# Row factors by transposes, idle transposes in a second place, and forget rates from quarters of the array, in a two-layer decoder on one Trainium2 core

## The chip, the cores and the metric

The kernel runs on one core of a Trainium2 chip. The core has a matrix engine (TensorE, "PE" in the profile, with its weight loads as "PEld"), a vector engine (DVE), an activation engine (ACT), a general engine (POOL) and a queue engine that issues transfers (SP). The metric is device time in microseconds of one execution, the lower the better. Three timed runs of the kernel before are shown, and one profiled execution.

## The reference

Two decoder layers over 256 positions of width 1024, float32 throughout. What matters here:

```
hn = rmsnorm(h, norm_mix_g[layer])        # every sublayer starts with one
h  = h + mixer(hn)                        # layer 0: stick-breaking + MoBA heads, layer 1: forgetting attention
h  = h + memory_cross_attention(rmsnorm(h), rmsnorm(mem))
h  = h + conv_ffn(rmsnorm(h))             # 1024 -> 2*2816, conv of width 3, silu gate, 2816 -> 1024
return rmsnorm(h)

# forgetting attention, layer 1: 16 forget rates per position come out of the same input projection
f_logit = proj[..., 3*D_MODEL:] + b_f     # (256 positions, 16 heads)
log_f   = log_sigmoid(f_logit);  c = cumsum(log_f)
s = q.k*scale + c[t] - c[s]
```

`rmsnorm(x, g) = x * rsqrt(mean(x*x) + 1e-6) * g`: one factor per position.

## The kernel before

**Layout.** h lies transposed: eight tiles `h[k]` of 128 features by 256 positions (two halves of 128). A product of a weight matrix with h is a projection of 24 matmuls: for each of the eight k-tiles, weights and activations are split into a high and a low part (`hi`, `lo`, a rounded float32 and its rest), and three products are summed, (hi, xh), (hi, xl), (lo, xh). Such a projection is `proj` (out has 128 features on the partitions) or `proj_nat` (positions on the partitions; the moving operand is then the weights). Operands of these matmuls have the type fp32r, one pass each. A plain float32 matmul is carried out as two passes, each with a weight load of its own, and shows as two instructions in the trace.

**Weights.** `block` (L119) loads 128x1024 weights (SP queue), rounds them on ACT (L127) and takes the rest on DVE (L128). PE's instructions stand in the order in which the code issues them; the order on the other engines comes from a scheduler that uses priorities.

**Row factors.** The norm is applied late: projections run on h times g alone, and their results are multiplied by the factor per position. `Stats.sums` (L254) sums squares over features with plain float32 matmuls of one column (L259), takes mean and epsilon (L262, DVE), and the power -0.5 on POOL (L266): the result is `rcol`, 128 positions by 2. It then builds a diagonal matrix `dg` from `rcol` with two DVE operations (L269). `Stats.spread` (L272) multiplies the diagonal by a matrix of ones with one plain float32 matmul of 256 columns (L274), so that every partition holds all 256 factors, and copies them to `row` (L277, ACT). Results are multiplied by `row` where they leave PSUM. There are seven spreads: at the start of layer 0, for the memory, and for cross attention and feed-forward network of both layers and the mixer of layer 1. Where a projection is given `hooks={n: f}`, f is issued behind its n-th product.

**Forget rates.** In layer 1, before q and k of the first group, L639 runs a `proj` with m=16: 24 matmuls of 16 output features. `decay_rows` (L493) turns them into cumulative sums, and each head loads its row from DRAM (`bc`).

**Feed-forward network** (`ffn`, L772): 22 pairs of up-projections, f = 0 to 21. The sums come behind product 6 of the first projection of f = 1, the spread behind product 12 of the second. Behind f = 1 stands `pace` (L522): six transposes of the identity into a spare PSUM bank whose result nobody reads. `renorm` (L775) makes normed activations `xn` (POOL, ACT, DVE) that replace raw ones from f = 4 (RAW) on. From f = 2 to the end of the up-projections PE runs 20 x 2 x 24 = 960 products, and in layer 0 another 8 x 66 = 528 of the down-projection behind them.

**Heads.** `visit(n)` issues a pair of heads at set ticks between projections: `heads_out` of pair n-2 (L418, outputs of 64 partitions per head), score products, `weigh` of pair n-1 (for softmax heads six transposes, L404), then the scores. `cross` issues its score products (L699, contraction over 64 rows per head) and outputs (L755, 64 partitions per head) in plain float32.

Of the kernel before, what the change touches and what calls it, by code (L numbers as in the profile page):

```python
# [72 lines left out]
def trunk(ctx: ExitStack, tc: tile.TileContext, a: dict, out: bass.AP):  # L73
# [145 lines left out]


    class Stats:
        def __init__(self, keep="", one=False):
# [31 lines left out]
        def sums(self):  # L254
            if self.ssq is None:
                ps = self.ps = bank(psA, "acc")
                for t in range(2):
                    for i, p in enumerate(self.parts):
                        nc.tensor.matmul(ps[:, 2 * t:2 * t + 1], p[:, t * P:(t + 1) * P], ones[:, 0:1], start=i == 0,  # L259
                                         stop=i == len(self.parts) - 1)  # L260
            ms = tiny.tile([P, 2], F32, tag="ms", name="ms")
            nc.vector.tensor_scalar(ms, ps[:, 0:4:2] if self.ssq is None else self.ssq, 1.0 / D, EPS, op0=ALU.mult,  # L262
                                    op1=ALU.add)
            bufs = 1 if self.keep else 2
            self.col = tiny.tile([P, 2], F32, tag="rcol" + self.keep, name="rcol", bufs=bufs)
            nc.gpsimd.tensor_tensor(self.col, ms, half, op=ALU.pow)  # L266
            self.dg = tmp.tile([P, T], F32, tag="diag", name="diag", bufs=1)
            for t in range(2):
                nc.vector.tensor_scalar(self.dg[:, t * P:(t + 1) * P], ident, self.col[:, t:t + 1], None, op0=ALU.mult)  # L269


        def spread(self, ps=None):  # L272
            ps = ps or self.ps
            nc.tensor.matmul(ps[:, :T], ones, self.dg, start=True, stop=True)  # L274
            bufs = 1 if self.keep else 2
            self.row = act.tile([P, T], F32, tag="rrow" + self.keep, name="rrow", bufs=bufs)
            nc.scalar.copy(self.row, ps[:, :T])  # L277


    def proj(b, off, xs, ps, first=True, last=True, m=P, hooks={}):  # L280
        n = 0
        for k, (xh, xl) in enumerate(xs):
            s = slice(off + k * m, off + k * m + m)
            end = last and k == len(xs) - 1
            for w, x in ((b.hi, xh), (b.hi, xl), (b.lo, xh)):
                nc.tensor.matmul(ps[:m], w[:, s], x, start=first and n == 0, stop=end and w is b.lo)  # L286
                n += 1
                if n in hooks:
                    hooks[n]()
        return ps  # L290

# [201 lines left out]
    def decay_rows(ps, st):  # L493
        f = lambda n: xin.tile([P, T], F32, tag="gh", name=n, bufs=NG)[:16]
        x, e, u, w, one, c = (f(f"f{n}") for n in "xeuw1c")
        nc.gpsimd.memset(one, 1.0)
        nc.vector.tensor_mul(x, ps[:16], st.row[:16])
        nc.vector.tensor_scalar(x, x, small[:16, C_BF:C_BF + 1], None, op0=ALU.add)
# [20 lines left out]
        return rows  # L519


    def pace():  # L522
        ps = bank(psO, "po")
        for i in range(6):
            nc.tensor.transpose(ps[:, (i % 4) * P:(i % 4 + 1) * P], ident, ident)

# [26 lines left out]
    def mixer(layer, st, xs):  # L553
# [14 lines left out]
        def visit(n):  # L568
            if n >= 2:
                outs[n - 2] = heads_out(heads[n - 2], pairs[n - 2][2], (n % 2) * P)  # L570
            if layer == 0:
                if n == 2:
                    rope_tables()
            if n < 8:
                q, k, _, rows = pairs[n]
                heads[n] = [Stick(i, q, k) if layer == 0 and n < 4 else Soft(i, q, k, rows[i]) for i in range(2)]
                both_products(heads[n])
            if 1 <= n < 9:
                for hd in heads[n - 1]:
                    hd.weigh()  # L580
            if n < 8:
                for hd in heads[n]:
                    hd.scores()
            if layer == 0 and n == 4:
                mem.sums()
            if layer == 0 and n == 5:
                mem.spread(accA())
            if layer == 0 and n == 1:
# [5 lines left out]
        for g in range(4):  # L594
# [43 lines left out]
            elif g == 0:  # L638
                f = proj(block(a["fox_f"], 8 * 16), 0, xs, bank(psO, "po", T), m=16)  # L639
                q, more = pair(0, ({3: st.sums}, {3: st.spread}))  # L640
                k = more()
                decay = decay_rows(f, st)
                q, k = evac_row(q, st, "q", True), evac_row(k, st, "k", False)
            else:
# [12 lines left out]
            for t in range(2):  # L657
                v.append(evac_col(proj_nat(b, xs, t, accA()), st, t, "v", 6))
                pipe.tick()
# [111 lines left out]

    def ffn(layer, st, xs):  # L772
        gs = []
        base = C_CONV + layer * 4 * 2 * KF
# [36 lines left out]
        for f in range(KF):  # L811
# [3 lines left out]
            for i in range(2):  # L815
                if f == 0:
                    pss.append(first[i])
                    continue
                hooks = ({6: st.sums}, {12: st.spread})[i] if f == 1 else {}
                acc = (accS, accA)[n % 7 % 2]()  # L820
# [8 lines left out]
            if f == 1:  # L829
                pace()  # L830
                renorm()
# [13 lines left out]
    def down_rows(gs):  # L845
# [21 lines left out]
        def finish(t):  # L867
            both = tiny.tile([P, 4], F32, tag="ssq", name="ssq")
            ms, col = both[:, 2:3], both[:, 3:4]
            for c in range(2):  # L870
                nc.scalar.activation(wide("sq"), acc[t][c], AF.Square, accum_out=both[:, c:c + 1])
            o = [wide("out") for _ in range(2)]
            if t:
                nc.vector.tensor_mul(o[0], acc[t][0], gain[0])
            nc.vector.tensor_add(ms, both[:, 0:1], both[:, 1:2])
            nc.vector.tensor_scalar(ms, ms, 1.0 / D, EPS, op0=ALU.mult, op1=ALU.add)
            nc.gpsimd.tensor_tensor(col, ms, half[:, 0:1], op=ALU.pow)
# [37 lines left out]
def _layout(inp):  # L915
# [27 lines left out]
    d["fox_in"] = qkv(fox[:, :3 * D])  # L943
    d["fox_f"] = c(kt(fox[:, 3 * D:]).reshape(P, -1))
    for n, w in (("ab_out", inp["ab_w_out"][0]), ("fox_out", inp["fox_w_out"][0])):
# [51 lines left out]
```

## Time and profile before

| what | value |
|---|---|
| timed runs | 671.16, 675.79, 671.14 us; median 671.16 us |
| profiled execution | 671.95 us, of which the span from the first to the last instruction is 670.2 us |
| PE busy | 660.1 us, 98% of the span |
| DVE, ACT, POOL busy | 528.5, 434.7, 60.0 us |
| mean granted TensorE clock | 0.997 of full speed |

In the rows below, a line of the timeline begins with its start in us, then its length, engine, source line (L286 is line 286 of the kernel), operation, output<-inputs by the program's names, shape and count. A matmul's length is its latency; what it costs PE in a stream is the time from one start to the next. A timeline row with x8 merges eight like instructions. In the chain of waits a piece is start, length and what ran, with its number of instructions.

### The profile page before, as it was taken

The numbers are of one execution on the slowest core, as the hardware profiler recorded it, in microseconds if no ns is written. First come the engines' busy times: TensorE is split into PE (matmuls) and PEld (weight loads), VectorE is DVE, ScalarE is ACT, GpSimd is POOL, SyncE is SP. The second block draws the span as 40 slices with busy tenths as digits, with TensorE's granted clock in tenths as the row PEclk, the third lists the DMA queues.
The fourth block names the chain that finished last, engine by engine and source line by source line (L and its number), as shares of the span: only waits on it lengthen the run. The fifth ranks groups of instructions, "written<-read, shape, count | busy, mean of one in ns | idle before, by whom it ended". The sixth has DMA issues, their size and how long they took to land.

```text
span 670.2 us, 14201 instructions
## 1 busy us (share of the span) xinstructions
PE 660.1 (98%) x5467; PEld 630.6 (94%) x5467; DVE 528.5 (79%) x1086; ACT 434.7 (65%) x864; POOL 60.0 (9%) x72
## 2 busy tenths in 40 slices
PE   8999999999999999999999999999999999999996
PEld 6999999989999999999999999999999999998884
DVE  5877995899999999766486787578999999994442
ACT  6699774767777776544464686567776777763332
POOL 0001110306100000011100000021350000000000
PEclk9999999999999999999999999999999999999998
DMA  8976451545455665665558554326356666654501
GB/s 293 400 270 227 130 205 34 187 158 184 147 200 197 217 219 174 185 190 181 192 186 268 188 173 132 126 76 208 88 197 215 193 219 205 207 193 151 191 0 64
DMA packets 39076, 121.83 MB, mean 182 GB/s; under 512 B 4944, under 2 KB 8928, under 8 KB 39008
## 3 DMA queue, kind: packets, MB, share of 16 engines
q1 hardware_dynamic: 38720, 120.62, 54.8%
q8 instruction: 43, 0.70, 0.4%
q10 hardware_dynamic: 288, 0.30, 0.1%
q14 instruction: 25, 0.20, 0.1%
HBM read 118.79 MB, written 1.06 MB: 179 GB/s over the span
## 4 chain that ended last, share of the span: by engine, by line
PE 91%; DVE 4%; issue 2%; DMA 1%; ACT 1%; SPq 0%; POOLq 0%; POOL 0%; DVEq 0%
PE acc L286 40%; PE sc L286 24%; PE acc L300 7%; PE sc L861 4%; PE po L861 2%; PE acc L861 2%; DVE wlo L128 2%; PE po L418 2%; PE sc L619 1%; PE sc L377 1%; PE sc L404 1%; PE po L300 1%; DVE xl L179 1%; DMA raw<-ab_first 1%; PE sc L699 1%
## 5 line engine op out<-in xcount | busy, mean ns | idle before, releaser
L128 DVE TENSOR_TENSOR wlo<-raw,whi 128x512 fp32r<-128x512 f32 (+2 forms) x285 | 262.2, 939 | 61.7 <-ACT whi L127 59.4
L127 ACT ACTIVATE whi<-raw 128x512 fp32r<-128x512 f32 (+2 forms) x285 | 225.2, 821 | 105.8 <-PE acc L286 46.4
L286 PE MATMUL sc<-xn,whi 128*128 128x256 f32 x672 | 116.1, 276 | 0.0
L286 PEld LDWEIGHTS sc<-xn,whi 128*128 128x128 f32 x672 | 101.3, 188 | 0.2
L286 PE MATMUL sc<-xn,wlo 128*128 128x256 f32 x336 | 92.7, 276 | 0.0
L286 PE MATMUL acc<-xn,whi 128*128 128x256 f32 x480 | 83.1, 276 | 0.0
L286 PE MATMUL acc<-xh,whi 128*128 128x256 f32 x288 | 81.8, 284 | 0.0
L286 PE MATMUL acc<-xl,whi 128*128 128x256 f32 x288 | 80.1, 278 | 0.0
L286 PE MATMUL acc<-xh,wlo 128*128 128x256 f32 x288 | 80.1, 278 | 0.0
L286 PEld LDWEIGHTS acc<-xn,whi 128*128 128x128 f32 x480 | 72.3, 188 | 0.0
L286 PE MATMUL acc<-gh,whi 128*128 128x256 f32 x240 | 67.2, 280 | 0.0
L286 PE MATMUL acc<-gl,whi 128*128 128x256 f32 x240 | 66.9, 279 | 0.1
L286 PE MATMUL acc<-gh,wlo 128*128 128x256 f32 x240 | 66.6, 277 | 0.0
L286 PE MATMUL acc<-xn,wlo 128*128 128x256 f32 x240 | 66.2, 276 | 0.0
L286 PEld LDWEIGHTS sc<-xn,wlo 128*128 128x128 f32 x336 | 63.1, 188 | 0.0
L234 POOL TENSOR_TENSOR sq<-sq 128x256 f32<-128x256 f32 x33 | 27.7, 838 | 328.1 <-ACT sq L228 313.5
L286 PEld LDWEIGHTS acc<-xl,whi 128*128 128x128 f32 x288 | 54.3, 189 | 0.1
L286 PEld LDWEIGHTS acc<-xh,whi 128*128 128x128 f32 x288 | 54.3, 188 | 0.2
L286 PEld LDWEIGHTS acc<-xh,wlo 128*128 128x128 f32 x288 | 54.2, 188 | 0.0
L286 PEld LDWEIGHTS acc<-gh,whi 128*128 128x128 f32 x240 | 45.2, 188 | 0.9 <-ACT gh L174 0.8
L286 PEld LDWEIGHTS acc<-gl,whi 128*128 128x128 f32 x240 | 45.1, 188 | 0.5 <-DVE gl L175 0.5
L286 PEld LDWEIGHTS acc<-gh,wlo 128*128 128x128 f32 x240 | 45.1, 188 | 0.0
(253 smaller groups left out, 1496.3 us busy)
## 6 DMA issues: line engine op xcount, KB each, us to landing
raw<-up SPq DMA_DIRECT2D x88, 512.0 KB, 4.3
raw<-fox_in SPq DMA_DIRECT2D x24, 512.0 KB, 4.2
raw<-down_rows SPq DMA_DIRECT2D x22, 512.0 KB, 4.3
raw<-ab_in SPq DMA_DIRECT2D x20, 512.0 KB, 6.7
raw<-down SPq DMA_DIRECT2D x16, 448.0 KB, 3.3
raw<-ab_out SPq DMA_DIRECT2D x8, 512.0 KB, 4.2
raw<-down SPq DMA_DIRECT2D x8, 512.0 KB, 3.6
raw<-fox_out SPq DMA_DIRECT2D x8, 512.0 KB, 3.4
```

Of the source, the lines that this page charges most:

```text
L127: i = nc.scalar.activation(hi[:, s], raw[:, s], AF.Copy)
L128: j = nc.vector.tensor_sub(lo[:, s], raw[:, s], hi[:, s].bitcast(F32))
L179: nc.vector.scalar_tensor_tensor(lo, src, g, hi.bitcast(F32), op0=ALU.mult, op1=ALU.subtract))
L234: nc.gpsimd.tensor_tensor(sq, sq, self.acc, op=ALU.add)
L286: nc.tensor.matmul(ps[:m], w[:, s], x, start=first and n == 0, stop=end and w is b.lo)
L300: nc.tensor.matmul(ps, x[:, s], y[:, w], start=n == 0, stop=n == 3 * KD - 1)
L377: nc.tensor.matmul(s[:, c], q[:, qs], k[:, 0:n], start=i == 0, stop=True, skip_group_check=True)
L404: nc.tensor.transpose(self.s[:, c:c + P], self.p[:, c:c + P], ident)
L418: nc.tensor.matmul(po[i * DH:(i + 1) * DH, q], v[m][:, vc + i * DH:vc + (i + 1) * DH], hd.pt[:, c], start=m == 0, stop=m == 1)
L619: nc.tensor.matmul(ps, wt[:, o + i * P:o + (i + 1) * P], x, start=start, stop=n == KD - 1 and wt is b.lo)
L699: nc.tensor.matmul(s[:, t * T:(t + 1) * T], self.q[:, t * P:(t + 1) * P], self.k, start=t == 0, stop=True, skip_group_check=True)
L861: nc.tensor.matmul(acc[t][c], x[:, s], y[:, c * 512:(c + 1) * 512], start=False, stop=k == KF - 1 and x is gl, skip_group_check=True)
```

## The change

It has these parts:

1. `sums` no longer builds the diagonal. `spread` issues two transposes of 128 columns: the stationary operand is a column of `rcol`, repeated over 128 columns, the moving one the identity. `turns(ps, n)` issues n idle transposes of the identity ahead of them: none in most places, two in the mixer of layer 1, four in the feed-forward networks.
2. In the feed-forward network the spread stands behind product 11 instead of 12, and `pace` (six idle transposes as before) behind product 21 of the same projection instead of behind its end.
3. The forget rates: weights `fw` (32 columns per k-tile, 16 of them zeros) are loaded once and multiplied by g during layer 0 (`gate_weights`); `gates` issues eight plain float32 matmuls of 32 output rows straight from h, the k-tile k going to rows 32*(k%4) of one PSUM bank, so that four quarters of the array's columns are used in turn. One ACT copy and three DVE additions sum the quarters. `gates` and then `sums` stand behind product 20 of q, the spread behind product 15 of k. The v results of the first group go to another PSUM pool (`accS`).
4. `rope_tables` moves behind `weigh` in its visit, the memory's spread ahead of `weigh` in its visit.
5. At the end, the mean's scale and epsilon are applied to the first half of the sum while the second is still made, and one fused operation follows in place of two.

```
+    def turns(ps, n):
+        for i in range(n):
+            c = slice(i % 2 * P, (i % 2 + 1) * P)
+            nc.tensor.transpose(ps[:, c], ident, ident)
+    def pace():
+        turns(bank(psO, "po", T), 6)
...
-            self.dg = tmp.tile([P, T], F32, tag="diag", name="diag", bufs=1)
-            for t in range(2):
-                nc.vector.tensor_scalar(self.dg[:, t * P:(t + 1) * P], ident, self.col[:, t:t + 1], None, op0=ALU.mult)
-        def spread(self, ps=None):
+        def spread(self, ps=None, idle=0):
             ps = ps or self.ps
-            nc.tensor.matmul(ps[:, :T], ones, self.dg, start=True, stop=True)
+            turns(ps[:, T:], idle)
+            for t in range(2):
+                nc.tensor.transpose(ps[:, t * P:(t + 1) * P], self.col[:, t:t + 1].broadcast_to([P, P]), ident)
...
+    fw = cst.tile([P, KD, 32], F32, name="fw")
+    def gate_weights():
+        nc.sync.dma_start(fw, a["fox_f"])
+        g = small[:, G_MIX + KD:G_MIX + 2 * KD]
+        nc.vector.tensor_tensor(fw, fw, g.unsqueeze(2).broadcast_to([P, KD, 32]), op=ALU.mult)
+    def gates(ps):
+        for k in range(KD):
+            j = 32 * (k % 4)
+            nc.tensor.matmul(ps[j:j + 32], fw[:, k], h[k], start=k < 4, stop=k > 3, skip_group_check=True)
...
-        nc.vector.tensor_mul(x, ps[:16], st.row[:16])
+        nc.scalar.copy(x, ps[:16])
+        for j in (32, 64, 96):
+            nc.vector.tensor_add(x, ps[j:j + 16], x)
+        nc.vector.tensor_mul(x, x, st.row[:16])
...
-                f = proj(block(a["fox_f"], 8 * 16), 0, xs, bank(psO, "po", T), m=16)
-                q, more = pair(0, ({3: st.sums}, {3: st.spread}))
+                f = bank(psO, "po", T)
+                def rates():
+                    gates(f)
+                    st.sums()
+                q, more = pair(0, ({20: rates}, {15: lambda: st.spread(idle=2)}))
...
-                hooks = ({6: st.sums}, {12: st.spread})[i] if f == 1 else {}
+                hooks = ({6: st.sums}, {11: lambda: st.spread(idle=4), 21: pace})[i] if f == 1 else {}
...
             if f == 1:
-                pace()
                 renorm()
...
+            nc.vector.tensor_scalar(ms, both[:, 0:1], 1.0 / D, EPS, op0=ALU.mult, op1=ALU.add)
             if t:
                 nc.vector.tensor_mul(o[0], acc[t][0], gain[0])
-            nc.vector.tensor_add(ms, both[:, 0:1], both[:, 1:2])
-            nc.vector.tensor_scalar(ms, ms, 1.0 / D, EPS, op0=ALU.mult, op1=ALU.add)
+            nc.vector.scalar_tensor_tensor(ms, both[:, 1:2], 1.0 / D, ms, op0=ALU.mult, op1=ALU.add)
```

How instructions move, in three places. On PE at the start of layer 1's mixer, before (po is the bank of the forget rates, acc that of q, sq the squares):

```order
L286 MATMUL po<-xl,whi 16x256
L286 MATMUL po<-xh,wlo 16x256
L286 MATMUL acc<-xh,whi 128x256
L286 MATMUL acc<-xl,whi 128x256
L286 MATMUL acc<-xh,wlo 128x256
L259 MATMUL acc<-const,sq 128x1 x2
L286 MATMUL acc<-xh,whi 128x256
```

And with the change, 20 products into q:

```order
L295 MATMUL acc<-xl,whi 128x256
L313 MATMUL po<-h_97,fw 32x256 x2
L313 MATMUL po<-h_98,fw 32x256 x2
L313 MATMUL po<-h_99,fw 32x256 x2
L313 MATMUL po<-h_100,fw 32x256 x2
L268 MATMUL acc<-const,sq 128x1 x2
L295 MATMUL acc<-xh,wlo 128x256
```

The 24 matmuls ahead of q (the last two are seen above) are gone, and eight stand inside q, ahead of the sums.

On PE in a feed-forward network with the change, in the second projection of f = 1 (the x4 and x6 rows are idle transposes):

```order
L295 MATMUL acc<-xl,whi 128x256
L224 MATMUL acc<-const 128x128 x4
L283 MATMUL acc<-const,rcol 128x128 x2
L295 MATMUL acc<-xh,wlo 128x256
...
L224 MATMUL po<-const 128x128 x6
L295 MATMUL acc<-xh,whi 128x256
```

The first block of six replaces one L274 row; the row of x6 was behind the projection's last product and is now three products ahead of its end.

On DVE in the same network while `xn` is made, before (u and c belong to the convolution; the second xn row here is the last of the eight):

```order
L793 TENSOR_TENSOR u<-acc,rrow 128x256
L128 TENSOR_TENSOR wlo<-raw,whi 128x1024
L179 SCALAR_TENSOR_TENSOR xn<-hr,small,xn 128x256
L128 TENSOR_TENSOR wlo<-raw,whi 128x1024
L179 SCALAR_TENSOR_TENSOR xn<-hr,small,xn 128x256
```

And with the change:

```order
L820 TENSOR_TENSOR u<-acc,rrow 128x256
L128 TENSOR_TENSOR wlo<-raw,whi 128x1024
L179 SCALAR_TENSOR_TENSOR xn<-hr,small,xn 128x256 x2
L823 SCALAR_TENSOR_TENSOR c<-u,small,c 128x255 x2
L823 SCALAR_TENSOR_TENSOR c<-u,small,c 128x254
L179 SCALAR_TENSOR_TENSOR xn<-hr,small,xn 128x256
L823 SCALAR_TENSOR_TENSOR c<-u,small,c 128x254
L820 TENSOR_TENSOR u<-sc,rrow 128x256
L128 TENSOR_TENSOR wlo<-raw,whi 128x1024
```

The last xn stands ahead of a weight operation (L128) that it used to follow, and behind three short ones.

## Rows read from the trace of the kernel before

**Rows 1.** From the page: the span, PE's busy time, the granted clock in 40 slices (9 is full speed), and the chain that ended last, by engine.

```profile
span 670.2 us, 14201 instructions
...
PE 660.1 (98%) x5467; PEld 630.6 (94%) x5467; DVE 528.5 (79%) x1086; ACT 434.7 (65%) x864; POOL 60.0 (9%) x72
...
PEclk9999999999999999999999999999999999999998
...
PE 91%; DVE 4%; issue 2%; DMA 1%; ACT 1%; SPq 0%; POOLq 0%; POOL 0%; DVEq 0%
```

**Rows 2.** Pieces of the chain of waits in order of time: start, length, what ran, number of instructions.

```profile
273.32 59.84 PE acc L286 x528
333.16 2.72 PE po L286 x24
...
347.77 11.30 PE acc L286 x96
...
370.55 5.66 PE acc L286 x48
...
389.98 5.46 PE acc L286 x48
```

**Rows 3.** Timeline of PE in the feed-forward network of layer 0, around the spread and the idle transposes.

```profile
161.59 0.28 PE L286 MATMUL acc<-xh,wlo 128*128 128x256 f32 x1
161.71 0.59 PE L274 MATMUL acc<-diag,const 128*128 128x256 f32 x2
161.95 0.47 PE L286 MATMUL acc<-xh,whi 128*128 128x256 f32 x1
162.26 0.28 PE L286 MATMUL acc<-xl,whi 128*128 128x256 f32 x1
...
163.41 0.28 PE L286 MATMUL acc<-xh,wlo 128*128 128x256 f32 x1
163.53 0.82 PE L525 MATMUL po<-const 128*128 128x128 f32 x6
164.11 0.37 PE L286 MATMUL sc<-xh,whi 128*128 128x256 f32 x1
164.31 0.28 PE L286 MATMUL sc<-xl,whi 128*128 128x256 f32 x1
```

**Rows 4.** Timeline of PE in cross attention of layer 0, around the spread.

```profile
132.81 0.28 PE L286 MATMUL sc<-xh,whi 128*128 128x256 f32 x1
132.96 0.70 PE L274 MATMUL acc<-diag,const 128*128 128x256 f32 x2
...
133.62 0.28 PE L286 MATMUL sc<-xh,wlo 128*128 128x256 f32 x1
```

**Rows 5.** Timeline of PE in cross attention: plain float32 matmuls on two halves of the array's rows (L699) and of its columns (L755).

```profile
134.91 0.28 PE L300 MATMUL po<-wlo,gh 128*128 128x256 f32 x1
135.12 2.00 PE L699 MATMUL sc<-mk,mq 64*128 64x256 f32 x16
137.05 0.38 PE L300 MATMUL po<-whi,gl 128*128 128x256 f32 x1
...
143.36 1.08 PE L755 MATMUL po<-xpt,mv 128*64 128x256 f32 x8
144.27 1.03 PE L755 MATMUL acc<-xpt,mv 128*64 128x256 f32 x8
```

**Rows 6.** Timelines of PE, DVE and POOL in the mixer of layer 1: the sums and what follows until the diagonal.

```profile
336.06 0.50 PE L259 MATMUL acc<-const,sq 128*128 128x1 f32 x4
...
337.04 0.14 DVE L262 TENSOR_SCALAR ms<-acc 128x2 f32<-128x2 f32 x1
...
338.38 0.48 DVE L269 TENSOR_SCALAR diag<-const,rcol 128x128 f32<-128x128 f32 x2 [0.60 <-POOL rcol L266]
...
337.26 1.08 POOL L266 TENSOR_TENSOR rcol<-ms,half 128x2 f32<-128x2 f32 x1 [1.90 <-DVE ms L262]
```

**Rows 7.** Timelines of PE and DVE in layer 0's feed-forward network where the last normed tile is first used.

```profile
177.35 0.28 PE L286 MATMUL sc<-xn,wlo 128*128 128x256 f32 x1
177.47 0.54 PE L286 MATMUL sc<-xn,whi 128*128 128x256 f32 x2
177.85 0.28 PE L286 MATMUL sc<-xn,wlo 128*128 128x256 f32 x1
...
175.97 1.21 DVE L128 TENSOR_TENSOR wlo<-raw,whi 128x1024 fp32r<-128x1024 f32 x1
177.10 0.47 DVE L179 SCALAR_TENSOR_TENSOR xn<-hr,small,xn 128x256 fp32r<-128x256 f32 x1
```

**Rows 8.** Timeline of DVE at the end of the program.

```profile
664.53 0.16 DVE L875 TENSOR_TENSOR ssq<-ssq 128x1 f32<-128x1 f32 x1 [2.12 <-ACT sq L871]
664.72 0.15 DVE L876 TENSOR_SCALAR ssq<-ssq 128x1 f32<-128x1 f32 x1
```

**Rows 9.** Timelines of SP (the first loads of the heads' decay rows) and of DVE (their first use).

```profile
350.28 1.28 SPq L516 DMA_DIRECT2D bc<-decay  x3
...
360.87 0.41 DVE L393 CUSTOM_DVE_ANT_0 s<-sc,bc 128x256 f32<-128x256 f32 x1
```

**Rows 10.** Busy time by stretch (us; PE, PEld, DVE, ACT, POOL, then the granted clock, DMA share and GB/s): sixteen transposes of cross attention, and the six idle ones.

```profile
141.50:143.30 1.80, 1.80 (x18) 1.69 (x16) 1.45 (x5) 1.80 (x4) 0.00 (x0) 1.00 0.00 0
...
163.50:164.10 0.60, 0.60 (x8) 0.60 (x7) 0.60 (x3) 0.00 (x0) 0.60 (x1) 1.00 0.95 389
```

More of the change, by code (lines that the diff above doesn't have):

```diff
@@ L266, in sums @@
             nc.gpsimd.tensor_tensor(self.col, ms, half, op=ALU.pow)
-            self.dg = tmp.tile([P, T], F32, tag="diag", name="diag", bufs=1)
+        def spread(self, ps=None, idle=0):
+            ps = ps or self.ps
+            turns(ps[:, T:], idle)
             for t in range(2):
-                nc.vector.tensor_scalar(self.dg[:, t * P:(t + 1) * P], ident, self.col[:, t:t + 1], None, op0=ALU.mult)
-        def spread(self, ps=None):
-            ps = ps or self.ps
-            nc.tensor.matmul(ps[:, :T], ones, self.dg, start=True, stop=True)
+                nc.tensor.transpose(ps[:, t * P:(t + 1) * P], self.col[:, t:t + 1].broadcast_to([P, P]), ident)
             bufs = 1 if self.keep else 2
@@ L289, in proj @@
                     hooks[n]()
+        return ps
+    fw = cst.tile([P, KD, 32], F32, name="fw")
[7 more added lines that the diff above has]
+            nc.tensor.matmul(ps[j:j + 32], fw[:, k], h[k], start=k < 4, stop=k > 3, skip_group_check=True)
         return ps
@@ L519, in decay_rows @@
         return rows
[L522 to L525, printed above, removed]
     def residual(j, ps, stats, nxt):
@@ L570, in visit @@
                 outs[n - 2] = heads_out(heads[n - 2], pairs[n - 2][2], (n % 2) * P)
-            if layer == 0:
-                if n == 2:
-                    rope_tables()
             if n < 8:
@@ L577, in visit @@
                 both_products(heads[n])
+            if layer == 0 and n == 5:
+                mem.spread(accA())
             if 1 <= n < 9:
@@ L580, in visit @@
                     hd.weigh()
+            if layer == 0 and n == 2:
+                rope_tables()
             if n < 8:
@@ L585, in visit @@
                 mem.sums()
-            if layer == 0 and n == 5:
-                mem.spread(accA())
             if layer == 0 and n == 1:
@@ L638, in mixer @@
             elif g == 0:
-                f = proj(block(a["fox_f"], 8 * 16), 0, xs, bank(psO, "po", T), m=16)
-                q, more = pair(0, ({3: st.sums}, {3: st.spread}))
+                f = bank(psO, "po", T)
[3 more added lines that the diff above has]
+                q, more = pair(0, ({20: rates}, {15: lambda: st.spread(idle=2)}))
                 k = more()
+                q, k = evac_row(q, st, "q", True), evac_row(k, st, "k", False)
                 decay = decay_rows(f, st)
-                q, k = evac_row(q, st, "q", True), evac_row(k, st, "k", False)
             else:
@@ L657, in mixer @@
             for t in range(2):
-                v.append(evac_col(proj_nat(b, xs, t, accA()), st, t, "v", 6))
+                v.append(evac_col(proj_nat(b, xs, t, (accA if g else accS)()), st, t, "v", 6))
                 pipe.tick()
@@ L772, in ffn @@
     def ffn(layer, st, xs):
+        if layer == 0:
+            gate_weights()
         gs = []
@@ L943, in _layout @@
     d["fox_in"] = qkv(fox[:, :3 * D])
-    d["fox_f"] = c(kt(fox[:, 3 * D:]).reshape(P, -1))
+    f = np.zeros((P, KD, 32), np.float32)
+    f[:, :, :16] = kt(fox[:, 3 * D:])
+    d["fox_f"] = f
     for n, w in (("ab_out", inp["ab_w_out"][0]), ("fox_out", inp["fox_w_out"][0])):
```

## The prediction

> **What bounds the kernel now.** I read the page first: PE is busy 660.1 of 670.2 us, the chain that ended last is 91% PE, and the granted clock is at full speed all the way [rows 1]. DVE's 79% and ACT's 65% are averages of engines that feed PE; DVE has only 4% of the chain. So a change is worth what it takes off PE's own stream, plus the few places where PE waits. The chain in order of time then shows what a product costs: 59.84 us for 528, that is 113.3 ns each, in the long feed-forward stretch, but 11.30 us for 96, or 117.7 ns, at 347.77, with the same shapes at the same clock [rows 2]. PE's stream has **two paces**, 4.4 ns apart, and which one it takes is settled where something else stands between products: two stretches behind the same kind of head block run at 5.66/48 = 117.9 and 5.46/48 = 113.8 ns [rows 2]. I found no rule in the rows that says which comes out. This is the largest unknown here. Last I read the PE timelines around the touched places.
>
> **Forget rates.** Removed: 24 products, 2.72 us of PE, on the path [rows 2]. Added: eight float32 matmuls, 16 passes. No row shows quarters of the columns; the nearest are halves. Eight passes on two column halves take 144.27 - 143.36 = 0.91 us from first start to the next group's, that is four rounds of 0.23 us in which two passes run side by side [rows 5]. If four run side by side, 16 passes are again four rounds, 0.91 us. Entering costs 135.12 - 134.91 = 0.21 us where an ordinary step is 0.12, so 0.09 more; leaving costs 137.05 - 135.12 = 1.93 less eight rounds (1.82), 0.11 more [rows 5]. Together 1.11. If only pairs run side by side it is 1.82 + 0.20 = 2.02, and one after the other 3.64 + 0.20 = 3.84; below 0.91 nothing, since every column quarter has four passes of its own. I take 1.11, because the halves overlap completely and the quarters differ from them by number alone. The term is -2.72 + 1.11 = **-1.61**. The Trainium skill, TensorE: Matmul & The Clock Gate, section "Why this matters for your kernels", gives 2.38 times for three column tiles and 3.07 for four row tiles, less than full overlap; by 3.07 the 3.64 us would shrink to 1.19 instead of 0.91, and the sum below would be 0.28 us smaller. No row here shows quarters.
>
> **Spreads.** Before, the diagonal's matmul costs 162.26 - 161.59 = 0.67 us between two products that would be 0.23 apart: 0.44 [rows 3]. In cross attention it is 133.62 - 132.81 = 0.81, so 0.58 [rows 4]. Six transposes between products cost 164.31 - 163.41 = 0.90, so 0.67; one more or less is (0.82 - 0.27)/5 = 0.11, the last one's latency of about 0.27 taken off; two then cost 0.23 and four 0.45 [rows 3]. So:
> - start of layer 0, and the memory's spread: 0.23 for 0.44, -0.21 each;
> - cross attention, two layers: 0.23 for 0.58, -0.35 each;
> - mixer of layer 1, with two idle ones: 0.45 for 0.44, nothing;
> - feed-forward networks, with four idle ones: 0.67 for 0.44, +0.23 each.
>
> That is -0.42 - 0.70 + 0.46 = **-0.66**. The repeated column as stationary operand is new; its weight load could be as long as an ordinary one (bound +0.1 in all) or no longer than the identity's. `pace` costs its 0.67 before and after. Moving it, and the ten products between the two sets, can itself bring at most 10 x 4.4 ns per layer, 0.09 us together; I count nothing.
>
> **Waits.** In the feed-forward network PE waits for the last normed tile: 177.85 - 177.35 = 0.50 us for three products' 0.34, 0.16 lost, and DVE makes that tile (177.10) only behind a weight operation of 1.21 us [rows 7]. With the change it stands ahead of that operation, behind three short ones. The tile comes some 0.8 us earlier, the wait goes in both layers: **-0.32**, bound 0. Next late there would be that weight operation itself, whose block is used a whole projection later. The factor must be there before the spread: in the mixer of layer 1 POOL ends at 338.34, 2.28 us behind the first sum at 336.06 [rows 6]. Now 19 products lie between, 17 of them behind the restart: 0.56 + 17 x 0.113 = 2.5 us, and two idle turns add 0.22. The cover is 0.4 us; without it PE stands still for what is missing, 0 to 0.3. In the other places the two diagonal steps (0.48 on DVE [rows 6]) are gone from between, so nothing becomes later.
>
> **What is hidden.** Fourteen DVE operations of the diagonals go (seven times 0.48 us), as do a small load and its casts; one load of 128 KB and one DVE operation of 128x256 come into layer 0, where PE's queue has no wait for DVE. The rates gain an ACT copy and three DVE additions, each no longer than the 0.41 us of a wider operation [rows 9], 1.6 us at worst, and one more weight load stands ahead of the decay rows on SP. Decay rows are first asked for at 350.28 and first used at 360.87, 10.6 us later [rows 9]; that covers both, even with PE 1.6 us earlier. `rope_tables` moves within its visit and costs the same four transposes. At the end one of two dependent DVE steps goes: 664.72 - 664.53, **-0.19** [rows 8], with all of the tail behind it.
>
> **Sum.** -1.61 - 0.66 - 0.32 - 0.19 = -2.78 us. Against the profiled execution that is 671.95 - 2.78 = 669.2; that execution lay 0.79 above the median of the runs shown, 671.16, and against the median it is **668.4 us**.
>
> **Rivals.**
> 1. *The long runs fall to the slow pace (slower than before).* The idle transposes are the last thing that stands between products before the feed-forward stretch. Before, what came out behind them was the quick pace [rows 2, 3]. Their place and what precedes them change, and `fw` shifts the tiles behind it by a kilobyte per partition. The stretch is 960 + 528 products in layer 0 and 960 in layer 1; at 4.4 ns that is 6.5 and 4.2 us: 672.6 with layer 1 alone, 674.9 with layer 0 alone, 679.1 with both. It beats the saving from some 630 products on. For it: the pace is sticky, and one of the three runs shown lay 4.6 us above the others, about the size of layer 1's stretch. Against: the six transposes came out quick in this trace, and the operand order behind them is the same. Chance 0.12.
> 2. *Quarters do not all overlap.* Then 0.91 us is lost in pairs (669.3), 2.73 one by one (671.1): no gain left in the last case. For it: no row has quarters. Against: both kinds of halves overlap completely. Chance 0.13.
> 3. *The short stretches turn quick.* Behind the touched places lie about five slow stretches no longer than the 96 products at 347.77 [rows 2]; all of them would give 5 x 96 x 4.4 ns = 2.1 us, half of them 1.0: 666.3 to 667.4. For it: transposes replace the two-pass matmul at each. Against: transposes leave both paces behind. Chance 0.12.
> 4. *The clock drops over the idle turns.* Sixteen transposes in a row, and the six, passed at a granted clock of 1.00, the 2.4 GHz level [rows 10]. The ten products between the sets at half speed would cost 1.1 us per layer, 670.6. Chance 0.01. This rival is what the Trainium skill, TensorE: Matmul & The Clock Gate, section "PE-mode transpose", would make of it: transposes do not count as work for the clock in the same way. The trace does not bear that out.
> 5. *The factor comes late in the mixer of layer 1*, or the xn wait stays: 668.7 to 669.0, inside the forecast's own range.
>
> **How the numbers follow.** The forecast, 667.4 to 669.2 with its own bounds, has 0.62. The range has to take in rival 2, half of rival 3 and rival 1 in layer 1 alone: 666.7 to 672.7, leaving out about 0.15. About 1% (6.7 us) is what a measurement of this kernel can tell from no change. Faster than that, under 664.4, would need nearly every slow stretch to turn quick besides the sum: 0.03. Slower, over 677.9, needs both long runs slow: 0.05. Within 1%: 0.92.
>
> **What would show it.** In the changed profile: the gap between products around the new float32 matmuls, 1.2 us if right, 2.1 or more if rival 2 holds; 0.46 us over the cross-attention spreads and 0.9 over each set of six turns; no step over 0.12 us where the last xn is first used; and the pace of the long stretches, 113.3 ns, in both layers. The prediction is wrong if a long stretch reads 117.7, if PE waits ahead of the col transposes, or if the chain leaves PE for more than the tail.

## The result, and the profile after

The changed kernel takes **669.63 us**, the median of 20 runs (668.44 to 674.27). The kernel before, run beside it 20 times, has a median of 675.75 us (671.14 to 682.66): two of its three runs that were shown ahead of the prediction lay at the low end. The ratio is 0.9924 [0.9901, 0.9947], within 1%; it leaves out runs more than 1.5% above the fastest of the same kernel, here the three of the kernel before at 682 us and more. The new time lies 1.2 us above the 668.4 that was predicted. The two profiled executions differ by less, 671.95 to 669.63 us.

So there are two differences, 6.1 us between the medians and 2.3 between the profiles. All runs of the kernel before in this study, 107 with those of the later comparisons, explain the first. They stand in four groups with empty space between them:

| times of the kernel before, us | runs | middle of the group | above the lowest |
|---|---|---|---|
| 670.95 to 672.92 | 39 | 671.7 | |
| 674.64 to 676.58 | 32 | 675.5 | 3.8 |
| 677.36 to 678.66 | 23 | 678.1 | 6.3 |
| 680.71 to 682.66 | 13 | 682.1 | 10.4 |

The prediction worked out what a long stretch at the slow pace costs: 4.2 us in layer 1, 6.5 in layer 0, 10.7 in both. The steps of the table lie 0.2 to 0.4 us below these. Of the changed kernel's 20 runs, 16 lie from 668.44 to 670.17 and four from 672.92 to 674.27: the first two groups, and nothing above. From lowest group to lowest group (medians 671.88 and 669.57 in the 20 runs) the change brings 2.3 us; the rest of the difference, read by these steps, is how often a long stretch comes out slow.

Now the profile after, by the prediction's steps. First PE's timeline over the forget rates (L313), to be read against [rows 5]:

```profile
335.52 0.28 PE L295 MATMUL acc<-xl,whi 128*128 128x256 f32 x1
335.73 1.07 PE L313 MATMUL po<-h,fw 128*32 128x256 f32 x16
336.73 0.61 PE L268 MATMUL acc<-const,sq 128*128 128x1 f32 x4
```

All 16 passes fit between 335.52 and 336.73: a gap of 1.21 us. Inside the merged row the starts come in fours, the four of a round within 21 ns, and the second, third and fourth round begin 0.240, 0.215 and 0.216 us after the one before. The quarters run side by side.

PE's timeline around the spread by transposes (L283) in cross attention, against [rows 4], and in layer 0's feed-forward network with both sets of idle turns (L224), against [rows 3]:

```profile
133.47 0.28 PE L295 MATMUL sc<-xh,whi 128*128 128x256 f32 x1
133.59 0.38 PE L283 MATMUL acc<-const,rcol 128*128 128x128 f32 x2
133.72 0.36 PE L295 MATMUL sc<-xl,whi 128*128 128x256 f32 x1
133.92 0.28 PE L295 MATMUL sc<-xh,wlo 128*128 128x256 f32 x1
...
161.78 0.28 PE L295 MATMUL acc<-xl,whi 128*128 128x256 f32 x1
161.90 0.60 PE L224 MATMUL acc<-const 128*128 128x128 f32 x4
162.34 0.38 PE L283 MATMUL acc<-const,rcol 128*128 128x128 f32 x2
162.47 0.37 PE L295 MATMUL acc<-xh,wlo 128*128 128x256 f32 x1
162.68 0.28 PE L295 MATMUL acc<-xh,whi 128*128 128x256 f32 x1
...
163.59 0.28 PE L295 MATMUL acc<-xh,wlo 128*128 128x256 f32 x1
163.71 0.82 PE L224 MATMUL po<-const 128*128 128x128 f32 x6
164.29 0.37 PE L295 MATMUL acc<-xh,whi 128*128 128x256 f32 x1
164.49 0.28 PE L295 MATMUL acc<-xl,whi 128*128 128x256 f32 x1
```

Two products over the cross-attention spread take 133.92 - 133.47 = 0.45 us (0.81 before), and each set of six transposes 0.90: 162.68 - 161.78 and 164.49 - 163.59.

Where the last normed tile is first used, DVE has it ready earlier than [rows 7] showed, with no weight operation directly ahead of it:

```profile
174.24 1.26 DVE L823 SCALAR_TENSOR_TENSOR c<-u,small,c 128x255 f32<-128x255 f32 x3
175.43 0.47 DVE L179 SCALAR_TENSOR_TENSOR xn<-hr,small,xn 128x256 fp32r<-128x256 f32 x1
```

It is done at 175.90. PE's first product with normed tiles starts at 175.61 and the last tile is asked for 21 products later, at 178.0: 2.1 us of cover, where before it came too late. No step there is over 0.12 us, in either layer. At the end of the program DVE's one step starts at 662.40 and POOL's power at 662.64, 0.24 us where the two steps of [rows 8] took 0.43.

What the prediction did not have is in PE's waits in all of the program past 5 us (who waited for whom, us in total, times, longest) of the kernel before, and then of the changed kernel:

```profile
PE sc L619 <- ACT whi L207: 1.9, 2, 1.8
PE sc L377 <- DVE k L490: 0.2, 1, 0.2
...
PE sc L401 <- DVE k L514: 2.3, 3, 1.6
PE sc L639 <- ACT whi L207: 0.6, 1, 0.6
```

In layer 0's mixer PE waits three times for DVE's rotated keys, 2.3 us in all; before it was once, 0.2. DVE's timeline ahead of the first of them:

```profile
65.59 0.42 DVE L308 TENSOR_TENSOR fw<-fw,small 128x256 f32<-128x256 f32 x1 [2.87 <-DMA fw<-fox_f]
65.93 0.55 DVE L376 SCALAR_TENSOR_TENSOR s<-sc,s 128x384 f32<-128x384 f32 x1
```

The chain of waits runs through the same place, and reaches PE again where the last and longest of the three waits (1.6 us) ends. Its shares by engine, first, were 91% PE, 4% DVE and 1% DMA before [rows 1]:

```profile
PE 78%; DVE 10%; DMA 5%; ACT 3%; issue 2%; POOL 0%; POOLq 0%; DVEq 0%; SPq 0%; ACTq 0%
...
57.25 8.32 DMA fw<-fox_f
65.93 0.56 DVE s L376
...
101.62 0.43 DVE k L514
102.19 0.92 PE sc L401 x8
```

The scaling of the forget-rate weights is written in the feed-forward network, but nothing ties it there, and the scheduler put it into DVE's queue in the mixer. Its load needs 8.32 us. The view of the transfers from 50 to 68 us, in 40 slices of 0.45 us, shows the DMA engines 90% busy or more nearly all the while that it is under way (from the 17th slice to the 35th):

```profile
DMA  0000001122027398997999999999999999421000
```

DVE stands 2.87 us, and all that feeds the next heads stands behind it.

### The profile page after: what moved, and what is told of

The parts are those of the page before. It is cut to its first block, busy times and chain, and to the rows that moved or that the text cites. A ratio compares the mean times of both kernels' runs of the same rounds, so it can differ in the third digit from the quotient of the medians.

```text
span 667.8 us, 14202 instructions
## 1 busy us (share of the span) xinstructions
PE 657.1 (98%) x5469; PEld 627.7 (94%) x5469; DVE 528.3 (79%) x1074; ACT 434.7 (65%) x863; POOL 59.6 (9%) x72
## 4 chain that ended last, share of the span: by engine, by line
PE 78%; DVE 10%; DMA 5%; ACT 3%; issue 2%; POOL 0%; POOLq 0%; DVEq 0%; SPq 0%; ACTq 0%
PE acc L295 35%; PE sc L295 24%; DVE wlo L128 4%; PE sc L887 4%; PE acc L324 3%; PE po L887 2%; PE acc L887 2%; DMA raw<-xt 1%; DMA fw<-fox_f 1%; PE po L442 1%; PE sc L401 1%; PE sc L428 1%; DVE xl L179 1%; ACT whi L127 1%; PE po L324 1%
## 5 line engine op out<-in xcount | busy, mean ns | idle before, releaser
L128 DVE TENSOR_TENSOR wlo<-raw,whi 128x512 fp32r<-128x512 f32 (+2 forms) x283 | 261.1, 943 | 62.0 <-ACT whi L127 59.8
```

What stands on the lines that cost most here:

```text
L128: j = nc.vector.tensor_sub(lo[:, s], raw[:, s], hi[:, s].bitcast(F32))
```

## The experiments

**Theories.** A: the idle turns settle the pace of the long stretches. B: the wait for the last normed tile draws the pace anew, and its going is what counts. C: the scatter comes from transfers. D: DVE's wait for the forget-rate weights costs PE its three waits; E: PE would wait there anyway.

### The two sets of turns, one at a time

The changed kernel without either set:

```diff
-hooks = ({6: st.sums}, {11: lambda: st.spread(idle=4), 21: pace})[i] if f == 1 else {}
+hooks = ({6: st.sums}, {11: st.spread})[i] if f == 1 else {}
```

> The changed kernel without either set of idle turns in the feed-forward networks (neither the four ahead of the spread nor the six ten products later); outputs stay the reference's. Theory A (the turns settle PE's pace in the long stretches, and the 671 to 683 of the kernel before is that pace coming out differently): the work falls by 0.67 + 0.45 us per layer, 2.2 in all, so 667.4 where both long stretches run at 113.3 ns, and steps of +4.2 (layer 1 at 117.8), +6.5 (layer 0) and +10.7 (both) above it in many executions; the median above 671, the scatter 4 us or more. Theory B (the wait for the last normed tile redrew the pace behind the turns; it is gone with the spread by transposes, whatever the turns do): median 667.4, at least three quarters of the executions within 1 us of it. Theory C (the scatter comes from transfers at the start, not from PE): 667.4 with the same scatter as the changed kernel, and no long stretch at 117.8 in the trace.

Measured: 671.67 us (668.07 to 679.05, 12 runs; ratio 0.9954 [0.9923, 0.9985]). Nine runs lie from 668.07 to 671.77, of which one is at 668.07 and eight from 670.50 up, one at 673.23, two at 679. With only the first set (`{11: lambda: st.spread(idle=4)}`):

> The changed kernel with the four idle turns ahead of the spread and without the six ten products later; outputs stay the reference's. 0.67 us of work less per layer, 1.34 in all. Theory A, with the second set as the part that repairs what the spread leaves (in the trace of the changed kernel layer 1 ran 8 products at 117.9 between the two sets and at 113.3 behind the second): 668.3 where both stretches are quick, but layer 1 at 117.8 in most executions, so a median near 672.5. Theory B: 668.3, little scatter.

Measured: 679.49 us (672.86 to 680.74; 1.0053 [1.0017, 1.0089]): nine of 12 runs at 679.0 or more. Both theories missed this: A had layer 1 alone slow and 672.5, B little scatter at 668.3. With only the second (`{11: st.spread, 21: pace}`):

> The changed kernel with the six turns ten products behind the spread and without the four ahead of it; outputs stay the reference's. 0.45 us of work less per layer, 0.9 in all. Theory A with the second set deciding: 668.7, one execution in five at +4.2, as the changed kernel has it. If the first set matters as well: steps of +4.2 or +6.5 in more than half of the executions, median above 672. Theory B: 668.7, little scatter.

Measured: 672.54 us (668.47 to 679.25; 0.9955 [0.9922, 0.9988]): four of 12 runs from 668.47 to 668.95, seven from 672.12 to 674.25, one at 679.25. A piece of the chain of waits in layer 0, and one in layer 1, first without turns, then with the first set alone:

```profile
272.42 62.11 PE acc L295 x548
...
497.88 5.65 PE sc L295 x48
```

```profile
277.20 64.54 PE acc L295 x548
```

62.11/548 is 113.3 ns, 64.54/548 117.8, 5.65/48 117.7. So the groups of times are the pace, and C is out. Neither set does it alone: the first alone is the worst of all, and layer 1 is slow in most runs of the other two. The pair is more than its parts, which is more than theory A said.

These profiles also bear on B. With either set alone no step where the last normed tile is first used is over 0.13 us, in either layer: the wait is gone. Yet both layers are slow with the first set alone, and layer 1 with the second. So the wait's going does not bring the quick pace by itself. Without turns the wait was not gone in layer 0, against what the expectation took for granted (0.54 us for two products, 0.31 lost), and the pace behind it stayed quick:

```profile
176.39 0.70 PE L295 MATMUL sc<-xn,whi 128*128 128x256 f32 x2
176.93 0.29 PE L295 MATMUL sc<-xn,wlo 128*128 128x256 f32 x1
```

### The scaling out of DVE's way

```diff
+        g = tiny.tile([P, KD], F32, name="gl8", bufs=1)
+        nc.vector.scalar_tensor_tensor(g, st.row[:, :KD], 0.0, small[:, G_MIX + KD:G_MIX + 2 * KD], op0=ALU.mult, op1=ALU.add)
...
-        if layer == 0:
-            gate_weights()
...
+            if f == 8 and layer == 0:
+                gate_weights(st)
```

> The changed kernel with the scaling of the forget-rate weights tied to the feed-forward network's row factor, so that DVE does it inside the feed-forward network of layer 0 and not in the mixer, where DVE stood 2.87 us for the load of these weights; the load itself stays where it was; outputs stay the reference's. Theory D (that wait delays DVE by 0.6 to 0.9 us and PE pays for it where it waits 2.3 us for rotated keys at three heads' scores): those waits fall to between 0.2 and 1.6 us and the time to 667.4 to 669.0. Rival E (PE came 1 us earlier and DVE, which sets the pace of that stage, would make it wait all the same): waits still near 2 us, 669.3 to 669.7.

Measured: **668.00 us** (667.73 to 669.33, 7 runs; 0.9913 [0.9879, 0.9948]). PE's waits past 5 us are gone altogether, that for the keys as well as that at the start. The multiplication now stands at 191.5, where nobody waits for it. D holds: the time is inside its range, and the waits fell further than it said. It is 1.6 us between lowest groups (the kernel before has its lowest group at the same place in both comparisons, 671.9 and 671.8). The waits were 2.3 us, but in this profile 145 more products of the short stretches stand at the slow pace than in that of the changed kernel, 0.6 us. Its median is below that of either kernel; it was not run beside the changed kernel in one comparison.

### The parts on the kernel before

Both sets of turns alone, with the diagonal kept (`{11: lambda: st.spread(idle=4), 21: pace}`, and the `pace` behind the loop removed):

> The kernel before with both sets of idle turns in the feed-forward networks (four ahead of the spread, which stays a product with the diagonal, six ten products later) and nothing else of the change; outputs stay the reference's. The four turns add 0.45 us per layer, 0.9 in all: 672.1 where both long stretches run at 113.3 ns (the kernel before has its lowest group of times near 671.3). Theory A (the two sets together bring the quick pace, whatever the spread is made of): at least three quarters of the executions at 672 to 673, the rest 4.2 above. Theory F (the pace depends on the exact instructions ahead, so the sets work with the transposed spread only): groups at +4.2, +6.5 and +10.7 as in the kernel before, median above 675.

Measured: 672.54 us (671.40 to 673.20; 0.9974 [0.9953, 0.9995]), 12 of 12 in the lowest group, where in the same comparison 20 of 29 runs of the kernel before stand above it. So the two sets bring the quick pace with the spread as a product, too, and F is out. But this kernel has no wait for the last normed tile either: the scheduler put that tile earlier here too. So it does not tell A from B.

The forget rates alone, with the late scaling (`fw`, `gates`, the additions and the packing of the change, `{20: rates}, {15: st.spread}`):

> The kernel before with the forget rates of the change (quarters of the columns, their place inside the first projection's last products, the added copies) and nothing else; the scaling of their weights is done inside the feed-forward network of layer 0, as in the run that tied it to the row factor; outputs stay the reference's. Theory G (the term is what the trace shows: 24 products out, a step of 1.2 us in, 1.5 us less): each of the four groups of times 1.5 lower, 669.7 for the lowest; the groups' shares as before, since nothing near the feed-forward networks changed, so a median between 672 and 676. Theory H (the forget rates also take part in the narrow scatter): three quarters of the executions within 1 us of the lowest.

Measured: 674.32 us (669.77 to 680.36; 0.9987 [0.9953, 1.0021]). Three runs at 669.77 to 670.57, six from 673.40 to 676.36, three at 679.12 or more. The lowest group is at 670.50, and that of the kernel before in the same comparison at 672.14: 1.6 us less. The scatter stays, so G holds and H does not.

All eight products on one quarter:

```diff
-            j = 32 * (k % 4)
-            nc.tensor.matmul(ps[j:j + 32], fw[:, k], h[k], start=k < 4, stop=k > 3, skip_group_check=True)
+            nc.tensor.matmul(ps[0:32], fw[:, k], h[k], start=k == 0, stop=k == KD - 1)
```

> The changed kernel with the late scaling, and all eight products of the forget rates on the same 32 columns, summed there; the three additions over the quarters are left out, since nothing is left to add; outputs stay the reference's. If the four passes that start within 7 ns of each other in the trace of the changed kernel really run side by side (a round of four in 0.215 us): 16 passes one after the other take 3.4 us for 0.9, so the time is 2.6 us longer, 670.6 against 668.0. If a single pass takes half of a round (0.107 us) when it is alone: 0.9 us longer, 668.9.

Measured: 671.68 us (671.15 to 675.72, 10 runs; 0.9958 [0.9927, 0.9988]), eight of them up to 671.85. PE's timeline:

```profile
333.79 0.28 PE L295 MATMUL acc<-xl,whi 128*128 128x256 f32 x1
333.99 3.64 PE L313 MATMUL po<-h,fw 128*32 128x256 f32 x16
337.56 0.60 PE L268 MATMUL acc<-const,sq 128*128 128x1 f32 x4
```

From first pass to the next group it is 3.57 us, against 336.73 - 335.73 = 1.00 with quarters: 2.57 more, as expected. The time rose by 3.7, not by 2.6; about 0.4 of the rest is the comparison's level (the lowest group of the kernel before is 672.1 there) and 0.5 short stretches at the slow pace, 111 products more of them in this profile. The last 0.2 us have no account.

### Where the kernel before turns slow

The kernel before, unchanged, three more profiles:

> The kernel before, unchanged, for a second profile. If its groups of times are the pace of the long stretches (theory A): the profiled time is near 671.5 with both at 113.3 ns, near 675.5 with layer 1 at 117.8, near 678 with layer 0 at 117.8, or near 682 with both. If its times come from elsewhere (theory C): a time above 674 with both stretches at 113.3 ns.

> The kernel before, unchanged, for a third profile. Theory A: near 671.5 with both long stretches at 113.3 ns, near 675.5 with layer 1 at 117.8, near 678 with layer 0, near 682 with both. Theory C: a time above 674 with both stretches at 113.3 ns.

> The kernel before, unchanged, for a fourth profile. Theory A: near 671.5 with both long stretches at 113.3 ns, near 675.5 with layer 1 at 117.8, near 678 with layer 0, near 682 with both. Theory C: a time above 674 with both stretches at 113.3 ns.

Measured: 672.09, 678.44 and 681.59 us, one run each. The first has both long stretches at 113.3 ns. The second has layer 0 slow, the third both. The chain of waits of the second in layer 0, then PE's timeline at the wait:

```profile
167.33 2.72 PE acc L286 x24
...
181.21 2.83 PE acc L286 x24
...
277.32 62.19 PE acc L286 x528
```

```profile
177.59 0.28 PE L286 MATMUL sc<-xn,wlo 128*128 128x256 f32 x1
177.70 0.56 PE L286 MATMUL sc<-xn,whi 128*128 128x256 f32 x2
178.11 0.28 PE L286 MATMUL sc<-xn,wlo 128*128 128x256 f32 x1
178.22 0.40 PE L286 MATMUL sc<-xn,whi 128*128 128x256 f32 x2
178.46 0.28 PE L286 MATMUL sc<-xn,wlo 128*128 128x256 f32 x1
178.57 0.40 PE L286 MATMUL sc<-xn,whi 128*128 128x256 f32 x2
```

The six turns left the quick pace: 24 products take 2.72 us. At 177.70 PE waits for the last normed tile as in [rows 7], and behind that gap of 0.41 us every product takes 117.8 ns, for 1370 products. At 4.4 ns that is 6.0 us behind a wait that is itself 0.18 us long. The third profile shows the same at the same place in layer 0. In layer 1 it shows the other way in, the pace behind the six turns:

```profile
495.22 0.28 PE L286 MATMUL acc<-xh,wlo 128*128 128x256 f32 x1
495.34 0.82 PE L525 MATMUL po<-const 128*128 128x128 f32 x6
495.91 0.36 PE L286 MATMUL sc<-xh,whi 128*128 128x256 f32 x1
496.11 0.28 PE L286 MATMUL sc<-xl,whi 128*128 128x256 f32 x1
496.23 0.28 PE L286 MATMUL sc<-xh,wlo 128*128 128x256 f32 x1
496.35 0.28 PE L286 MATMUL sc<-xh,whi 128*128 128x256 f32 x1
```

The products ran at 117.9 ns ahead of the turns and go on so behind them. If the wait turns the pace, it does so by chance: in the profiles with such a wait in layer 0 the quick pace went on behind it four times and turned slow twice, and in layer 1 it went on all four times.

### Fewer turns, and the wait put back

Two turns in each set, on the kernel with the late scaling (`idle=2`, `turns(bank(psO, "po", T), 2)`):

> The changed kernel with the late scaling, and two idle turns instead of four ahead of the spread and two instead of six ten products later; outputs stay the reference's. Six turns less per layer at 0.11 us, 1.3 us less work in all. If it is the two interruptions that bring the quick pace, whatever their length: 666.7 in three quarters of the executions or more. If their length matters: groups of times 4.2, 6.5 or 10.7 above that, median above 670.

Measured: 670.76 us (667.02 to 671.90; 0.9955 [0.9926, 0.9984]): three of 12 runs up to 667.56, nine 3.5 to 5 us higher. Where the pace is quick the time is about 0.9 us below the late scaling's, of 1.3 expected, but by the times layer 1 is slow in most runs. In the profile layer 1 came to the second set at the quick pace (starts 113 to 114 ns apart) and left it at the slow one (117 to 119). So two interruptions of whatever length are not enough.

Four DVE steps ahead of the last normed tile, to bring the wait back behind both sets:

```diff
+                for _ in range(4 if k == KD - 1 else 0):
+                    nc.vector.tensor_scalar(t, t, 1.0, None, op0=ALU.mult)
```

> The changed kernel with the late scaling and all idle turns, and four added DVE steps (each a multiplication by one) ahead of the last normed tile of both feed-forward networks, so that this tile lands some 4 us later and PE waits for it again, by an estimate 0.2 us, as in the kernel before; outputs stay the reference's. Theory B (the wait draws the pace anew: in two profiles of the kernel before the long stretch of layer 0 ran 114 products at 113.3 ns up to it and 1370 at 117.8 behind it): besides the wait's own 0.2 to 0.5 us, a third or more of the executions stand 4.2, 6.5 or 10.7 above the lowest group, 6.5 among them, which no run with both sets of turns has shown. Theory A (the turns alone decide): at least four in five executions between 668.0 and 669.5, none at +6.5.

Measured: 667.89 us (667.12 to 668.72, 6 runs; 0.9879 [0.9842, 0.9917]). The experiment missed its aim. The tile lands at 176.62 and PE asks for it at 176.92, so there is no wait in either layer, and the run says nothing on B. It shows only that DVE has that much room there.

## Why the prediction came out as it did

The number was inside its range and the forecast's sign and class were right, but it was near for partly wrong reasons. Part of it is luck: two amounts outside the forecast, +2.1 and -1.7 us, nearly cancel, and two of the three runs it started from came from the lowest group. From the median of the 20 runs the same -2.78 would have given 673.0, outside the range. And one of its own signs of being wrong came up in the profile: the chain leaves PE for more than the tail, from the load of `fw` on. (Another, a long stretch at 117.7 ns, did not in this profile; by the times it did in four of the 20 runs.) By its steps:

- **Forget rates: right.** The gap was to be 1.2 us and is 1.21; against the ordinary step of 0.12 that is 1.09 added for 2.72 removed, -1.63 where -1.61 stood, and alone on the kernel before it brought 1.6. Rival 2, quarters that do not all overlap, is out: one quarter takes 3.57 us for 1.00 from the first pass to the next group, 3.6 times, and 3.77 for 1.21 with the step in front, 3.1 times. The Trainium skill (TensorE: Matmul & The Clock Gate, "Why this matters for your kernels") gives 3.07 for four row tiles; the column quarters here reach that with the step in front counted, and more without it.
- **Spreads: right** at each place: 0.45 us in cross attention for 0.46 expected, 0.90 for each set in the feed-forward networks, where PE's lag against the profile before grew by 0.21 and 0.25 for 0.23. In the mixer of layer 1 the factor was there 1.0 us ahead of its transposes (POOL's power from 337.63 for 1.08, transposes at 339.73) where 0.4 was forecast, so the first half of rival 5 is out; the wait for the last normed tile, its other half, is gone.
- **The tail: right**, 0.19.
- **The wait for the last normed tile: right.** It is gone in both layers, and PE's lag against the profile before falls there by 0.16 and 0.17 us, as the -0.32 had it. What the step did not ask is which pace comes out behind the wait: two other profiles of the kernel before turn slow there, for 6.0 us. That the wait is the cause is not shown.
- **"I count nothing" for the move of `pace`: wrong.** The step priced the ten products between the two sets, 0.09 us. What the sets bear on is which pace the 960 + 528 and the 960 products behind them take. I had this as rival 1, with the right sizes, but only as a loss from a quick profile. The kernel before was slow in one of the two layers or both in 68 of 107 runs, so there was more to gain than to lose, and one shown run in three, 4.6 us above the others, already said so. With both full sets, layer 0 was slow, by the times, in none of 55 runs (this kernel, the late scaling, one quarter, the added steps, and the turns alone) where before it was in 36 of 107, and layer 1 in 6, where before it was in 45. Dropping either set brings slow layers back, with no wait for the normed tile in the profiles, so it is the pair that matters there; none of the profiles with both sets has that wait, so what they would do with it is open.
- **"One DVE operation of 128x256 come into layer 0, where PE's queue has no wait for DVE": the failed step of the sum.** That operation waits for a load, and DVE feeds the heads' scores in the mixer. PE's waits there rose from 0.2 to 2.3 us, +2.1 where nothing stood. With the scaling moved the waits are gone and the time is 1.6 us shorter. The order of DVE's queue shows where the operation stands; the step does not ask for it.
- **Short stretches, rival 3: partly so, beside the forecast.** Counted from the starts of successive products, 745 of them are 115.5 to 121 ns apart, where it was 978; 233 at 4.4 ns are 1.0 us less. The stretches at 369 and 377, slow in [rows 2] and beside it, are quick here. But the same count is 1068 in the second profile of the kernel before and 890 with the late scaling, so how much of the 233 is the change's is open.
- **Rival 4, the clock: no.** Busy time by stretch over the first set, the ten products and the second (columns as in [rows 10]) has the granted clock at 1.00, the 2.4 GHz level, in all three:

```profile
161.90:162.40 0.50, 0.50 (x7) 0.50 (x6) 0.50 (x1) 0.00 (x0) 0.00 (x0) 1.00 0.91 270
162.50:163.60 1.10, 1.10 (x13) 1.10 (x10) 0.95 (x3) 0.37 (x1) 0.40 (x1) 1.00 0.80 246
163.80:164.30 0.50, 0.50 (x8) 0.50 (x6) 0.45 (x2) 0.32 (x1) 0.50 (x2) 1.00 0.96 377
```

Between the two profiles, in which the long stretches are quick both times, the sum closes: -2.78 forecast, +2.1 for the waits behind DVE, -1.0 for short stretches, and -0.7 at the start, where the first 96 products, which wait for their loads, ended 0.74 us earlier (that stretch took from 11.8 to 13.05 us in the profiles of all these kernels, so I give it no cause). That is -2.4, and -2.3 was measured.

**Open.** That the wait can turn the pace is suggested by two profiles and shown by no run in which the wait alone was added or removed: the run that was to add it did not, and a kernel before with the wait alone taken out was not tried. What decides the draw is not found either. In the profiles with both full sets the second set was entered at the slow pace in eight places and left at the quick one in all eight; without the four turns ahead it was entered slow twice and left slow twice. By the times, four of 20 runs of the changed kernel are slow in layer 1 all the same.

## What to carry to other kernels

Where runs of one kernel fall into groups, lay the distance between groups against (number of products) x (difference of two paces) before costing an edit, and take several profiles: the pace that a long stretch takes behind a short wait can cost thirty times the wait's own length. A new operation that depends only on a load can be placed by the scheduler far ahead of where the code has it (here in the mixer, two sublayers early), so look up its place in that engine's queue and what feeds on that engine there, and tie it to something late if it isn't wanted early. Small products with few output columns are cheap in quarters of the columns: 1.00 us here for 3.57.

## What was not expected of the hardware

Behind a gap of 0.41 us in a stream of equal products (two products and a wait of 0.18), each of 1370 products took 117.8 ns, where those ahead had taken 113.3, at a granted clock of 1.00 on both sides; behind eight other such gaps the pace stayed as it was. Four float32 passes on four column quarters started within 21 ns of one another and took rounds of 0.240, 0.215 and 0.216 us, start to start, as passes one by one on a single quarter do (0.240, then 0.215 to 0.216 each). A load of 128 KB took 8.32 us while the DMA engines were 90% busy or more with it and the loads beside it.
